# Zeros between the first transposes, one group's first block turned by VectorE, and biases loaded by SyncE: a matmul with bias and tanh

## The chip, the cores and the metric

The kernel runs on one core of one Trainium2 chip. The metric is the device time of one execution in microseconds (us), the median of several executions. One execution of each run was profiled; its **span**, from the first to the last instruction, is about 1.7 us shorter than the time. The **landing** of a transfer is the moment when all of its data has arrived; a **semaphore** is a counter by which a transfer or an engine tells others that it is done.

## The reference

```python
m, k, n = 4096, 4096, 4096
a, b, bias = randn(m, k), randn(k, n), randn(n)     # float32
out = np.tanh(np.matmul(a, b) + bias)
```

## The kernel before

a and b are read as float32 and cast to float16 by the transfer itself, which only GpSimd's queue issues here. TensorE needs a turned (k on the partitions). In the steady state VectorE turns it in 32x32 blocks; the loads put the right 32 partitions into the right place, so each such load is four transfers (`for q in (0, 2, 1, 3)`).

The beginning is built apart, so that TensorE has something to multiply soon. Eight blocks of 128 rows of a are worked on at once: group 0 (`g0`) and group 1 (`g1`), four blocks each, over a first stretch of k (4 rows of 128, `BL`), then a second (4 to 8), then a third (8 to 16). The blocks that are needed first are loaded naturally, one transfer each, and turned on TensorE against an identity matrix:

```python
def load_nat(m):                      # one transfer, 128 KB as float16
    ...
    nc.gpsimd.dma_start(out=nat, in_=src.rearrange("m (x t) -> m x t", t=BL))

def turn_nat(m, copy):                # four transposes, then a copy out of PSUM
    tp = psum.tile([P, BL, P], fp16, name="tp", tag="ps")
    for t in range(BL):
        nc.tensor.transpose(tp[:, t, :], nats[m][:, :, t], ident)
    copy(ats[m][:, ds(0, BL), :], tp)
```

PSUM is the memory that TensorE writes to. Before these transposes TensorE multiplies zeros nine times: they are meant to bring its clock from half to full early. Then (cut):

```python
turn_nat(0, nc.vector.tensor_copy)
turn_nat(1, nc.scalar.copy)
row(0, 0, 1)                          # block 0, first row of b: two matmuls
turn_nat(2, nc.vector.tensor_copy)
row(1, 0, 1)
row(2, 0, 1)
row(0, 1, 1)
...
load_nat(G)                           # group 1, blocks 0 and 1: natural
load_nat(G + 1)
want_a("g1a", 2, 6 * P, 2 * Q, 0, BL) # blocks 2 and 3: 4 transfers of 64 KB
want_a("g1b", G, 4 * P, G * Q, BL, BL)# second stretch of k: 4 of 128 KB
for i in range(BL):
    want(load_b_next)                 # second stretch of b: 4 of 256 KB
want_a("g0b", G, 0, G * Q, BL, BL)    # group 0, second stretch
want_a("g0c", G, 0, G * Q, KS, KM - KS)  # group 0, third stretch
```

`want` puts a load into a list, and at most three loads of a (`AN`) are under way or unturned at a time.

Of the kernel before, what the change touches and what calls it, by code (L numbers as in the profile page):

```python
# [14 lines left out]
P = 128  # L15
Q = 4
QP = 32
NB = 512
fp32 = mybir.dt.float32
# [4 lines left out]
def kernel(  # L24
# [7 lines left out]
    nc = tc.nc  # L32
# [6 lines left out]
    NCW = 1024  # L39
    NC = N // NCW  # L40
    J = NCW // NB
    TB = 4
    G = 4
    KS = 8
    AN = 3
    BL = 4
    KM = 16
    WARM = 9

    singles = ctx.enter_context(tc.tile_pool(name="singles", bufs=1))  # L50
    bpool = ctx.enter_context(tc.tile_pool(name="bpool", bufs=2))
# [4 lines left out]
    psum = ctx.enter_context(tc.tile_pool(name="psum", bufs=8, space=bass.MemoryType.PSUM))  # L56
# [4 lines left out]
    def new_b():  # L61
        return [
            bpool.tile([P, TB, NCW], fp16, name=f"b_{i}", tag=f"b_{i}") for i in range(KT // TB)
        ]
# [19 lines left out]
    def load_a(m0, nmb, t0, nt):  # L84
        an = anat.tile([P, nmb, nt * QP], fp16, name="an")
        for t, n in split(t0, nt):
            for q in (0, 2, 1, 3):
                k = t * P + q * BL * QP if t < KS else P * KS + (q * (KT - KS) + t - KS) * QP
                src = a[ds(m0, nmb * QP), ds(k, n * QP)]
                nc.gpsimd.dma_start(  # L90
                    out=an[ds(q * QP, QP), :, ds((t - t0) * QP, n * QP)],
                    in_=src.rearrange("(mb p) k -> p mb k", p=QP),
                )
        return an

    def transpose_a(at, an, mb0, t0, nt):

        for t, n in split(t0, nt):
            order = "P mb (k t) -> P mb t k" if t < KS else "P mb (t k) -> P mb t k"
            nc.vector.transpose(  # L100
                at[:, ds(t, n), :].rearrange("P t (mb p) -> P mb t p", p=QP),
                an[:, ds(mb0, Q), ds((t - t0) * QP, n * QP)].rearrange(order, k=QP),
            )

    def load_bias(bias_bc, n0, queue):
        src = bias[ds(n0, NCW)]
        queue.dma_start(
            out=bias_bc,
            in_=bass.AP(tensor=src.tensor, offset=src.offset, ap=[[0, P], *src.ap]),
        )  # L110
# [4 lines left out]
    def pump():  # L115
        while queue and (queue[0][0] is None or live[0] < AN):
            key, uses, load = queue.pop(0)
            made = load()
            if key is not None:
                live[0] += 1  # L120
                staged[key] = [made, uses]

    def want_a(key, uses, *where):
        queue.append((key, uses, lambda: load_a(*where)))

    def want(load):
        queue.append((None, 0, load))

    def turn(at, key, mb0, t0, nt):
        pump()  # L130
        transpose_a(at, staged[key][0], mb0, t0, nt)
        staged[key][1] -= 1
        if not staged[key][1]:
            live[0] -= 1
            pump()

    def mm(ps, at, bt, t, j, start, stop):
        nc.tensor.matmul(  # L138
            ps, at[:, t, :], bt[t // TB][:, t % TB, ts(j, NB)], start=start, stop=stop
        )  # L140

    def finish(ps, addend, mi, c0, w=NB, o_sb=None, queues=(nc.sync,)):
# [22 lines left out]
    ats = [  # L165
        bpool.tile([P, KT, P], fp16, name=f"atx_{m}", tag=f"b_{4 + m}") for m in range(G)
    ] + [atp.tile([P, KT, P], fp16, name="at") for m in range(G)]
# [24 lines left out]



    def one_by_one(ps, ms, t0, t1, first, before=None):
        for m in ms:
            if before:
                before(m)
            ps[m] = [psum.tile([P, NB], fp32, name="ps") for j in range(J)]
            for j in range(J):  # L200
                for t in range(t0, t1):
                    mm(ps[m][j], ats[m], b_cur, t, j, t == first, False)

    def across(ps, ms, t0, t1, first):
        for t in range(t0, t1):
            for m in ms:
                for j in range(J):
                    mm(ps[m][j], ats[m], b_cur, t, j, t == first, False)

    def down(ps, ms, t0, t1, done, before=None):  # L210
        for m in ms:
            if before:
                before(m)
            for j in range(J):
                for t in range(t0, t1):
                    mm(ps[m][j], ats[m], b_cur, t, j, False, t == t1 - 1)
                done(ps[m][j], m, j)

    g0, g1 = range(G), range(G, 2 * G)


    zeros = singles.tile([P, NB], fp16, name="zeros")
    ident = singles.tile([P, P], fp16, name="ident")
    nc.vector.memset(zeros, 0.0)  # L224
    nc.vector.memset(ident, 1.0)
    warm = psum.tile([P, NB], fp32, name="ps")
    for i in range(WARM):
        nc.tensor.matmul(warm, zeros[:, :P], zeros, start=i == 0, stop=i == WARM - 1)  # L228



# [6 lines left out]
    def load_nat(m):  # L238
        nat = opool.tile([P, P, BL], fp16, name="nat", tag="o_sb")
        src = a[ds(m * P, P), ds(0, P * BL)]  # L240
        nc.gpsimd.dma_start(out=nat, in_=src.rearrange("m (x t) -> m x t", t=BL))  # L241
        nats[m] = nat
# [6 lines left out]
    def turn_nat(m, copy):  # L249
# [4 lines that stand above are left out]
# [13 lines left out]
    ps = {}  # L267

    def row(m, t0, nt):
        if m not in ps:  # L270
            ps[m] = [psum.tile([P, NB], fp32, name="ps") for j in range(J)]
        across(ps, (m,), t0, t0 + nt, 0)

    turn_nat(0, nc.vector.tensor_copy)
    turn_nat(1, nc.scalar.copy)
    row(0, 0, 1)
    turn_nat(2, nc.vector.tensor_copy)
    row(1, 0, 1)
    row(2, 0, 1)
    row(0, 1, 1)  # L280
    row(1, 1, 1)
    turn_nat(3, nc.scalar.copy)
# [2 lines left out]
    across(ps, g0, 2, BL - 1, 0)  # L285


    load_nat(G)
    load_nat(G + 1)
    want_a("g1a", 2, 6 * P, 2 * Q, 0, BL)  # L290
    want_a("g1b", G, 4 * P, G * Q, BL, BL)
    for i in range(BL):
        want(load_b_next)
# [6 lines left out]
    bias_bc = biasp.tile([P, NCW], fp32, name="bias_bc")  # L300
# [8 lines left out]
    pump()  # L309


    def before0(m):
        if m == 3:
            turn_nat(G, nc.vector.tensor_copy)

    down(ps, g0, BL - 1, BL, put_aside, before0)

    def before1(m):
        if m == G + 1:
            turn_nat(m, nc.vector.tensor_copy)  # L320
            for i in range(2):
                turn(ats[G + 2 + i], "g1a", i * Q, 0, BL)
            for i in range(G):
                turn(ats[G + i], "g1b", i * Q, BL, BL)

    ps = {}
    one_by_one(ps, g1, 0, BL, 0, before1)
    across(ps, g1, BL, KS - 1, 0)
    for m in g0:
        turn(ats[m], "g0b", m * Q, BL, BL)  # L330
# [3 lines left out]
    ps = {}  # L334
# [11 lines left out]
    ps = {}  # L346
# [15 lines left out]
    def want_row(i):  # L362
        want_a(i, 1, todo[i][1] * P, Q, 0, KT)
# [9 lines left out]
    for m in g0:  # L373
        for j in range(J):
            ps = psum.tile([P, NB], fp32, name="ps")
# [10 lines left out]
    bias_next = None  # L386
    for i, (c, mi) in enumerate(todo):
        if mi == 0:
            b_cur, bias_bc = b_next, bias_next
        if c + 1 < NC and mi == (2 * G if c == 0 else 0):  # L390
            b_next = new_b()
            left = [(s, None) for s in range(KS // TB)]
            left += [(s, q) for s in range(KS // TB, KT // TB) for q in range(Q)]
        if i + ahead < len(todo):
            want_row(i + ahead)
        for s, q in left[:2]:
            if q is None:
                want(lambda s=s, c=c, bt=b_next: load_b_low(
                    nc.gpsimd, bt[s], (c + 1) * NCW, s * TB, TB))
            else:  # L400
                want(lambda s=s, q=q, c=c, bt=b_next: load_b(
                    bt, (c + 1) * NCW, s * TB, TB, q))
        left = left[2:]
        if c + 1 < NC and mi == MT - 4:
            bias_next = biasp.tile([P, NCW], fp32, name="bias_bc")
            want(lambda c=c, bb=bias_next: load_bias(bb, (c + 1) * NCW, nc.gpsimd))
        pump()
        if i + 2 < len(todo):
            new_at(i + 2)
        at = at_q.pop(0)  # L410
        for j in range(J):

            halves = 2 if i == len(todo) - 1 and j == J - 1 else 1
            w = NB // halves
            for h in range(halves):
                ps = psum.tile([P, w], fp32, name="ps")
                c0 = j * NB + h * w
                for t in range(KT):
                    nc.tensor.matmul(  # L419
                        ps,  # L420
                        at[:, t, :],
                        b_cur[t // TB][:, t % TB, ds(c0, w)],
                        start=t == 0,
                        stop=t == KT - 1,
                    )
                queues = (nc.sync, nc.scalar) if halves > 1 else (nc.sync,)
                finish(ps, bias_bc[:, ds(c0, w)], mi, c * NCW + c0, w, queues=queues)
# [30 lines left out]
```

## Time and profile before

| what | value |
|---|---|
| time, median of 3 executions | 1783.76 us (1782.66 to 1784.04) |
| span of the profiled one | 1782.8 us (its time was 1784.52, above all three) |
| TensorE busy | 1776.4 us |
| first matmul of group 1 | 16.74 us |
| its first on the second stretch of k | 24.58 us |
| first matmul of the main loop | 121.27 us |

The prediction below shows the lines of TensorE (start, busy us, engine, line, operation, how many; in brackets its idle time before and who ended it).

```profile
6.79 1.18 POOL L241 DMA_DIRECT2D nat<-in_a_dram  x2 [1.24 <-PE tp L252]
7.96 2.32 POOL L90 DMA_DIRECT2D an<-in_a_dram  x4
10.70 0.64 POOL L90 DMA_DIRECT2D an<-in_a_dram  x1 [0.43 <-DMA b<-in_b_dram]
11.95 2.08 POOL L90 DMA_DIRECT2D an<-in_a_dram  x3 [0.60 <-DMA b<-in_b_dram]
14.02 2.16 POOL L69 DMA_DIRECT2D b<-in_b_dram  x4
```

Between the last row of b of the first stretch (issued at 4.99) and the load of group 1's second stretch (from 10.70) stand six issues. Two of the brackets say that GpSimd waited for the *landing* of a row of b before it issued a piece of a that has nothing to do with b. And the work of all engines in stretches of 2 us (length; busy us of TensorE, its weight loads, VectorE, ScalarE and GpSimd, with the number of instructions in brackets; the share of the clock granted, the DMA share, and GB/s):

```profile
14.00:16.00 2.00, 2.00 (x13) 0.96 (x11) 0.00 (x0) 1.04 (x3) 2.00 (x5) 1.00 1.81 178
16.00:18.00 2.00, 1.91 (x12) 0.76 (x11) 0.42 (x1) 2.00 (x6) 2.00 (x4) 1.00 1.38 205
18.00:20.00 2.00, 1.48 (x10) 0.74 (x9) 1.10 (x3) 0.97 (x2) 0.77 (x2) 1.00 1.13 211
```

The transfers move 178 to 211 GB/s.

### The profile page before, as it was taken

What the parts mean: (1) busy time and instruction counts of PE and PEld (TensorE: products, weight loads), DVE (VectorE), ACT (ScalarE), POOL (GpSimd) and SP (SyncE); (2) the same over time, 40 slices, a digit from 0 to 9 for tenths busy, and PEclk for the clock granted to TensorE, in tenths of its full rate; (3) what the DMA queues carried; (4) which work ended last, traced back from release to release, by engine and by line L of the source; (5) the groups of instructions that cost most, each with busy time, mean ns of one, the idle gap of its engine ahead of it and who ended that gap; (6) DMA issues with size and microseconds to landing.
All of it is one profiled execution on the core that took longest, in us unless ns stands there. A gap on an engine that the chain in (4) does not pass through costs nothing.

```text
span 1782.8 us, 20849 instructions
## 1 busy us (share of the span) xinstructions
PE 1776.4 (100%) x8257; PEld 807.8 (45%) x8257; DVE 763.5 (43%) x679; ACT 173.2 (10%) x279; POOL 869.9 (49%) x1620
## 2 busy tenths in 40 slices
PE   9999999999999999999999999999999999999999
PEld 4444444444444444444444444444444444444444
DVE  2764443344434443444434443444334443444342
ACT  2021000000000000000000000000000000000001
POOL 7465556544466445444455554444544454444510
PEclk9999999999999999999999999999999999999999
DMA  9999999976999967767699987766777667766631
GB/s 188 201 184 175 169 162 167 138 133 107 159 168 163 161 109 117 119 109 128 112 167 173 167 142 117 120 116 107 129 116 122 107 112 117 119 114 109 117 77 42
DMA packets 280593, 238.68 MB, mean 134 GB/s; under 512 B 158000, under 2 KB 230960, under 8 KB 280496
## 3 DMA queue, kind: packets, MB, share of 16 engines
q0 software_dynamic: 243056, 169.71, 69.4%
q1 hardware_dynamic: 37152, 67.52, 10.6%
q8 instruction: 64, 1.05, 0.2%
q14 instruction: 33, 0.27, 0.0%
q10 hardware_dynamic: 288, 0.13, 0.0%
HBM read 337.64 MB, written 67.11 MB: 227 GB/s over the span
## 4 chain that ended last, share of the span: by engine, by line
PE 99%; DMA 0%; issue 0%; ACT 0%; DVE 0%; DVEq 0%; POOLq 0%
PE ps L419 93%; PE ps L138 6%; DMA nat<-in_a_dram 0%; PE tp L252 0%; ACT o_sb L152 0%; DVE at L253 0%; DVE o_sb L149 0%; ACT atx L253 0%; DVEq L149 0%; POOLq L442 0%
## 5 line engine op out<-in xcount | busy, mean ns | idle before, releaser
L419 PE MATMUL ps<-b,at 128*128 128x512 f16 x7712 | 1657.8, 378 | 0.0
L90 POOL DMA_DIRECT2D an<-in_a_dram x1488 | 800.2, 545 | 794.9 <-DVE at L100 562.4
L419 PEld LDWEIGHTS <-at 128*128 128x128 f16 x7712 | 754.6, 98 | 903.3
L100 DVE STREAM_TRANSPOSE at<-an 128x512 f16<-128x512 f16 (+1 forms) x378 | 564.0, 1543 | 54.9 <-DMA an<-in_a_dram 54.8
L149 DVE TENSOR_TENSOR o_sb<-ps,bias_bc 128x512 f32<-128x512 f32 (+1 forms) x243 | 165.9, 684 | 917.6 <-PE ps L419 712.3
L152 ACT ACTIVATE o_sb<-o_sb 128x512 f32<-128x512 f32 (+1 forms) x243 | 151.6, 625 | 1502.5 <-DVE o_sb L149 1496.2
L73 POOL DMA_DIRECT2D b<-in_b_dram x104 | 56.0, 541 | 20.6 <-DMA an<-in_a_dram 11.7
L138 PE MATMUL ps<-b,atx 128*128 128x512 f16 x256 | 57.7, 385 | 0.2 <-ACT atx L253 0.2
L138 PE MATMUL ps<-b,at 128*128 128x512 f16 x256 | 55.8, 379 | 0.6 <-DVE at L253 0.5
L138 PEld LDWEIGHTS <-at 128*128 128x128 f16 x256 | 24.9, 98 | 31.0 <-DVE at L253 1.3
L138 PEld LDWEIGHTS <-atx 128*128 128x128 f16 x256 | 25.0, 99 | 30.6 <-ACT atx L253 0.7
L100 DVE STREAM_TRANSPOSE atx<-an 128x512 f16<-128x512 f16 (+2 forms) x12 | 16.3, 1398 | 9.3 <-DMA an<-in_a_dram 9.3
L69 POOL DMA_DIRECT2D b<-in_b_dram x13 | 8.3, 643 | 20.1 <-PE ps L419 19.8
L152 ACT ACTIVATE spill<-spill 128x512 f32<-128x512 f32 x16 | 10.1, 629 | 81.8 <-DVE spill L149 81.8
L149 DVE TENSOR_TENSOR spill<-ps,spill 128x512 f32<-128x512 f32 x16 | 11.0, 686 | 13.3 <-PE ps L138 13.3
L181 DVE TENSOR_TENSOR spill<-spill,bias_bc 128x512 f32<-128x512 f32 x16 | 9.7, 677 | 0.0
L173 ACT COPY spill<-ps 128x512 f32<-128x512 f32 x16 | 8.0, 626 | 14.3 <-PE ps L138 14.3
L176 DVE TENSOR_TENSOR spill<-ps,spill 128x512 f32<-128x512 f32 x8 | 4.9, 681 | 4.0 <-PE ps L138 4.0
L228 PE MATMUL ps<-zeros 128*128 128x512 f16 x9 | 4.0, 631 | 1.3 <-DVE zeros L224 1.3
L253 DVE COPY at<-tp 128x512 f16<-128x512 f16 x2 | 0.8, 424 | 9.5 <-PE tp L252 9.5
L241 POOL DMA_DIRECT2D nat<-in_a_dram x6 | 3.4, 564 | 2.2 <-PE tp L252 1.2
L253 DVE COPY atx<-tp 128x512 f16<-128x512 f16 x2 | 0.8, 424 | 6.7 <-PE tp L252 6.7
(14 smaller groups left out, 13.3 us busy)
## 6 DMA issues: line engine op xcount, KB each, us to landing
an<-in_a_dram POOLq DMA_DIRECT2D x480, 192.0 KB, 4.9
out_dram<-o_sb SPq DMA_DIRECT2D x239, 256.0 KB, 2.5
an<-in_a_dram POOLq DMA_DIRECT2D x960, 32.0 KB, 2.6
b<-in_b_dram POOLq DMA_DIRECT2D x95, 256.0 KB, 8.1
b<-in_b_dram POOLq DMA_DIRECT2D x6, 1024.0 KB, 13.4
an<-in_a_dram POOLq DMA_DIRECT2D x32, 128.0 KB, 5.0
out_dram<-spill SPq DMA_DIRECT2D x16, 256.0 KB, 3.5
an<-in_a_dram POOLq DMA_DIRECT2D x12, 256.0 KB, 8.5
```

Of the source, the lines that this page charges most:

```text
L69: queue.dma_start(out=dst, in_=src[:, ds(t0 % BL, nt), :])
L73: nc.gpsimd.dma_start(out=bt[t0 // TB][ds(q * QP, QP), ds(t0 % TB, nt), :], in_=src.rearrange("(t p) n -> p t n", p=QP),)
L90: nc.gpsimd.dma_start(out=an[ds(q * QP, QP), :, ds((t - t0) * QP, n * QP)], in_=src.rearrange("(mb p) k -> p mb k", p=QP),)
L100: nc.vector.transpose(at[:, ds(t, n), :].rearrange("P t (mb p) -> P mb t p", p=QP), an[:, ds(mb0, Q), ds((t - t0) * QP, n * QP)].rearrange ...
L138: nc.tensor.matmul(ps, at[:, t, :], bt[t // TB][:, t % TB, ts(j, NB)], start=start, stop=stop)
L149: nc.vector.tensor_tensor(out=o_sb[:, piece], in0=ps[:, piece], in1=addend[:, piece], op=mybir.AluOpType.add)
L152: nc.scalar.activation(o_sb[:, piece], o_sb[:, piece], mybir.ActivationFunctionType.Tanh)
L173: nc.scalar.copy(aside(m, j), ps)
L176: nc.vector.tensor_tensor(out=aside(m, j), in0=ps, in1=aside(m, j), op=mybir.AluOpType.add)
L181: nc.vector.tensor_tensor(out=aside(m, j), in0=aside(m, j), in1=bias_bc[:, ts(j, NB)], op=mybir.AluOpType.add)
L228: nc.tensor.matmul(warm, zeros[:, :P], zeros, start=i == 0, stop=i == WARM - 1)
L419: nc.tensor.matmul(ps, at[:, t, :], b_cur[t // TB][:, t % TB, ds(c0, w)], start=t == 0, stop=t == KT - 1,)
```

## The change

Three things are meant. More zeros, also between the first transposes and matmuls, so that TensorE has no hole and its clock opens early. Group 1's first four blocks turned by VectorE out of two loads, so that TensorE loses no time to their transposes and to the copies after them. The three later biases loaded through SyncE's queue, the first of them in two halves.

```diff
-    WARM = 9
+    WARM = 11
...
+    def fill(n, w):
+        ps = psum.tile([P, NB], fp32, name="ps")
+        for i in range(n):
+            nc.tensor.matmul(
+                ps[:, ds(0, w)], zeros[:, :P], zeros[:, :w], start=i == 0, stop=i == n - 1
+            )
+    fill(WARM, NB)
...
     turn_nat(0, nc.vector.tensor_copy)
+    fill(3, P)
     turn_nat(1, nc.scalar.copy)
     row(0, 0, 1)
+    fill(2, P)
     turn_nat(2, nc.vector.tensor_copy)
     row(1, 0, 1)
+    fill(3, P)
     row(2, 0, 1)
+    fill(6, P)
     row(0, 1, 1)
...
-    load_nat(G)
-    load_nat(G + 1)
-    want_a("g1a", 2, 6 * P, 2 * Q, 0, BL)
+    want_a("g1a", 2, 4 * P, 2 * Q, 0, BL)
+    want_a("g1a2", 2, 6 * P, 2 * Q, 0, BL)
     want_a("g1b", G, 4 * P, G * Q, BL, BL)
...
+    for i in range(G):
+        turn(ats[G + i], "g1a2" if i > 1 else "g1a", i % 2 * Q, 0, BL)
     ...  (the two turn_nat between group 1's matmuls are gone)
-            want(lambda c=c, bb=bias_next: load_bias(bb, (c + 1) * NCW, nc.gpsimd))
+            for h in range(2 if c == 0 else 1):
+                w = NCW // (2 if c == 0 else 1)
+                load_bias(bias_next[:, ds(h * w, w)], (c + 1) * NCW + h * w, nc.sync)
```

More of the change, by code (lines that the diff above doesn't have):

```diff
@@ L105, in load_bias @@
     def load_bias(bias_bc, n0, queue):
-        src = bias[ds(n0, NCW)]
+        src = bias[ds(n0, bias_bc.shape[-1])]
         queue.dma_start(
@@ L190, in load_b_all, with one_by_one @@
             load_b(b_cur, 0, t0, nt, q)
-    def one_by_one(ps, ms, t0, t1, first, before=None):
+    def one_by_one(ps, ms, t0, t1, first):
         for m in ms:
-            if before:
-                before(m)
-            ps[m] = [psum.tile([P, NB], fp32, name="ps") for j in range(J)]
+            ps[m] = []
             for j in range(J):
+                ps[m].append(psum.tile([P, NB], fp32, name="ps"))
                 for t in range(t0, t1):
@@ L208, in across, with down @@
                     mm(ps[m][j], ats[m], b_cur, t, j, t == first, False)
-    def down(ps, ms, t0, t1, done, before=None):
+    def down(ps, ms, t0, t1, done):
         for m in ms:
-            if before:
-                before(m)
             for j in range(J):
@@ L225 @@
     nc.vector.memset(ident, 1.0)
-    warm = psum.tile([P, NB], fp32, name="ps")
-    for i in range(WARM):
-        nc.tensor.matmul(warm, zeros[:, :P], zeros, start=i == 0, stop=i == WARM - 1)
+    def fill(n, w):
[5 more added lines that the diff above has]
+    fill(WARM, NB)
     raw_b = spill[3].rearrange("P (t x) n -> P t (x n)", t=2)[:, ds(0, 1), :]
@@ L309 @@
     pump()
-    def before0(m):
-        if m == 3:
-            turn_nat(G, nc.vector.tensor_copy)
-    down(ps, g0, BL - 1, BL, put_aside, before0)
-    def before1(m):
-        if m == G + 1:
-            turn_nat(m, nc.vector.tensor_copy)
-            for i in range(2):
-                turn(ats[G + 2 + i], "g1a", i * Q, 0, BL)
-            for i in range(G):
-                turn(ats[G + i], "g1b", i * Q, BL, BL)
+    for i in range(G):
+        turn(ats[G + i], "g1a2" if i > 1 else "g1a", i % 2 * Q, 0, BL)
+    down(ps, g0, BL - 1, BL, put_aside)
+    for i in range(G):
+        turn(ats[G + i], "g1b", i * Q, BL, BL)
     ps = {}
-    one_by_one(ps, g1, 0, BL, 0, before1)
+    one_by_one(ps, g1, 0, BL, 0)
     across(ps, g1, BL, KS - 1, 0)
```

## The prediction

> **What bounds the kernel now.** I read the page from the top. TensorE is busy for 1776.4 of 1782.8 us, and the chain of waits that ended last is 99% TensorE.
>
> ```profile
> PE 1776.4 (100%) x8257; PEld 807.8 (45%) x8257; DVE 763.5 (43%) x679; ACT 173.2 (10%) x279; POOL 869.9 (49%) x1620
> ...
> PE 99%; DMA 0%; issue 0%; ACT 0%; DVE 0%; DVEq 0%; POOLq 0%
> ```
>
> So no transfer and no other engine can give much. Is there anything to win on TensorE itself? The chain in order of time answers (columns: start, length in us, what).
>
> ```profile
> 1.31 4.51 DMA nat<-in_a_dram
> ...
> 5.87 0.62 PE tp L252 x4
> ...
> 8.47 2.57 PE ps L138 x8
> ...
> 11.30 0.59 ACT atx L253
> ...
> 16.26 0.44 DVE at L253
> ...
> 18.90 0.43 DVE at L253
> ...
> 19.39 102.05 PE ps L138 x472
> 121.43 1654.20 PE ps L419 x7680
> ```
>
> From 19.39 us on TensorE never waits: 1654.20 us for 7680 matmuls is 215.4 ns each, and in the trace no matmul after 20 us starts more than 217 ns behind the one before it. The last 7.2 us (1775.6 to 1782.8) are the adds, tanh and stores of the last tile, which the change doesn't touch. The whole program has 8192 matmuls of the product (256 + 256 + 7680 and the few halves at the end), at 215.4 ns about 1765 us. With 5.87 us of waiting for the first block of a and 7.2 us of tail that is 1778 us; some 5 us at most lie in the beginning, and **only those can be won**. The TensorE timeline of the beginning (start, busy us, what, idle before):
>
> ```profile
> 1.26 4.02 PE L228 MATMUL ps<-zeros 128*128 128x512 f16 x9 [1.26 <-DVE zeros L224]
> 5.87 1.26 PE L252 MATMUL tp<-ident,nat 128*128 128x128 f16 x8 [0.59 <-DMA nat<-in_a_dram]
> ...
> 8.26 2.77 PE L138 MATMUL ps<-b,atx 128*128 128x512 f16 x8
> ...
> 11.94 4.06 PE L138 MATMUL ps<-b,atx 128*128 128x512 f16 x18 [0.25 <-ACT atx L253]
> 15.84 0.39 PE L252 MATMUL tp<-ident,nat 128*128 128x128 f16 x4
> 16.06 0.59 PE L138 MATMUL ps<-b,atx 128*128 128x512 f16 x2
> 16.74 1.90 PE L138 MATMUL ps<-b,at 128*128 128x512 f16 x8
> 18.48 0.39 PE L252 MATMUL tp<-ident,nat 128*128 128x128 f16 x4
> 19.39 12.26 PE L138 MATMUL ps<-b,at 128*128 128x512 f16 x56 [0.52 <-DVE at L253]
> ```
>
> Two losses are in it. First, speed: the 18 matmuls from 11.94 take 0.216 us each, the ones on zeros start 0.427 us apart, and single starts in the trace show the change of pace inside the matmul that starts at 9.97, near 10.06 us. All work between 5.87 and 10.06 ran at half pace. Second, group 1's first two blocks are turned on TensorE in the middle of the matmuls (15.84 and 18.48): four transposes each, then a wait for VectorE's copy out of PSUM.
>
> **What the Trainium skill says.** "TensorE: Matmul & The Clock Gate", section "What's actually happening": the array starts at half clock and gets the full one after a busy window of about 3.4 us; the window is free-running. The trace agrees: the pace doubles at 10.06, and the 3.41 us before it (6.65 to 10.06) have no gap, while the window before that (3.24 to 6.65) holds the hole from 5.08, where the last zeros stop streaming, to 5.87. Section "Wait — 56ns, not 53.3ns?": starts are 106.7 and 426.7 ns apart at N = 128 and 512 cold, 55.6 and 215.7 warm. The trace has 107 and 427, then 56 and 216. "VectorE: DVE Perf Modes", section "The three transpose paths": VectorE turns 32x32 blocks only, into SBUF. That is why the change also swaps the loads; the trace has 6 such turns of 128x512 in 3.67 us, 0.61 each, with no PSUM copy. "DMA: Bandwidth & Descriptors", section "Issuing engines are not separate DMA queues": another issuing engine saves only issue time. That bears on the bias.
>
> **The change part by part.** The order of instructions shows TensorE with 8 more pairs: +2 zeros of 512 columns, +14 of 128, -8 transposes. The rest of its order is the same.
>
> *Zeros.* Eleven at 0.427 from 1.26 end at 5.95, against the first block of a landing at 5.83: 0.08 us late, but no hole. The small ones stand where TensorE would wait for a landing or for a copy of a transpose (0.42 us on VectorE, 0.58 on ScalarE). With the same phase of the window, the window 3.24 to 6.65 is now busy throughout, so the full clock comes at about 6.65 instead of 10.06. I then walked the new order by hand with the landings of the trace before (blocks of a at 5.83, 6.47, 7.26, 9.16; rows of b at 8.52, 10.42, 11.66), the copies' durations, and about 0.05 us for a semaphore: transposes of block 0 5.95 to 6.38, zeros, block 1 6.68 to 6.90, first matmuls at 7.10 (the copy of block 0 ends at 7.05), block 2 at 7.64, block 1's matmuls 7.87, block 2's 8.55, six zeros from 8.98, then the second row of b at 9.31 against 9.97 before. The six zeros cost 0.33 us there, since that row has landed at 8.52. Block 3's copy by ScalarE still has to be waited for: its first matmul comes at about 11.23 against 11.94. **Saved: 0.7 us.**
>
> *Group 1 on VectorE.* From 11.23 there are 4 + 8 + 8 matmuls, 20 x 0.216 = 4.32 us, and group 1 starts at 15.55. Before it started at 16.74: the four transposes (4 x 0.056 = 0.22) and the wait (0.25) are gone, 0.48 us. The second block before cost from the end of the eighth matmul (18.48) to 19.39, 0.91 us. **Saved: 1.4 us**, if the turned blocks are ready. VectorE needs 0.61 us a block and is idle from 8.93. The loads are the question. The queue of GpSimd is full here, and landings come one behind the other at its pace: in the trace the last row of b at 11.66, the two blocks that go (128 KB each) at 12.32 and 13.10, the 64 KB pieces of the remaining load 0.38 us apart, to 14.47. The new loads are the same bytes in eight such pieces: 11.66 + 4 x 0.38 = 13.2 for the first two blocks, 14.7 for the others. Turned by 14.4 and 15.9; needed at 15.55 and, two blocks x 1.73 us later, at 19.0. Margin over one us.
>
> *What comes sooner must be fed sooner.* Group 1's second block of K: landed 17.50 before, needed at 15.55 + 32 x 0.216 = 22.5. Group 0's next load: 26.18, turned by 26.8, needed at 29.4. Its third: 31.41, turned from 32.7, needed at 36.3; the b for it lands by 33.97. Later b at 60.29, needed at 63.9; the load of a at 70.64, turned by 71.9, needed at 77.7. All hold with over a us, so the gain should reach the end.
>
> *Biases.* Three issues of 0.56 us leave GpSimd, which idles 794.9 us at its loads; four go to SyncE, which waits 1555 us for ScalarE. TensorE waits for neither: **0**.
>
> Sum: 24.57 before for the first matmul of group 1 on the second block of K, 22.46 after: 2.1 us off the profiled span, 1780.7.
>
> **The rivals.** (1) *The zeros bring no earlier clock*, because zeros of 128 columns or transposes count too little or a hole stays. Then 14 zeros at 0.107 are 1.5 us of load at half pace, part of it in gaps, and the zeros eat most of the gain: about 1783. For it: nothing in the trace shows zeros alone opening the clock. Against: the window 6.65 to 10.06 opened it with eight transposes' worth of time inside. (2) *The loads become the wait*: 32-partition pieces are issued at 0.58 us each, and each issue reuses a semaphore of an earlier DMA, so two of them wait for rows of b (10.42, 11.66). A late load of group 1 would put a DMA wait where the VectorE wait was, at 15.55 or 22.5; each us late costs one us, 1782 to 1783. Against: the queue's pace, not the issue, sets the landings there. (3) *The phase of the window favours the change more*: before, it can open anywhere from 9.3 to 12.7, after from 4.7 to 8.1. Walked by hand this moves before by -0.1 to +1.1 and after by only -0.3 to +0.5. For it: the three runs before spread over 1.4 us. The usual run before is then somewhat later than the profiled one, and the gain 2.5 to 2.8: 1781.0.
>
> **Range and chances.** 1783.76 - 2.1 = 1781.7 by the profiled phase, 1781.0 by the usual one; I take 1781.2. The low end is a gain of 3.7 (a late clock before in the median, an early one after), the high end 1.1 (rival 1 or 2 in part). Two per cent is 36 us, and the beginning holds about 5: anything but "within 2%" would need a fault elsewhere.
>
> **What would show it.** Weight loads about 0.22 us apart from about 6.7 us on; no idle TensorE between 1.3 and 5.9; no VectorE copies into group 1's tiles; group 1's first matmul near 15.6, with no wait before its second block; the first matmul of the main loop near 119.2 instead of 121.27; 215.4 ns a matmul there as before; no wait at L107. Wrong would be a DMA wait of TensorE at 15 to 30 us, or a pace of 0.43 us still at 9 us.

## The result

| | before | changed |
|---|---|---|
| time, median | 1783.80 us (1782.66 to 1784.04, 4 runs) | 1783.83 us (1783.25 to 1784.13, 4 runs) |
| ratio | | 1.0001, 95% interval 0.9984 to 1.0018 |
| span of the profiled run | 1782.8 | 1781.9 |

Ratios here are the mean time of one kernel's runs over that of the other's runs of the same rounds, so not quite the ratio of the medians quoted. The time stayed where it was; the predicted 1781.2, with a range of 1780.0 to 1782.7, was missed on the high side.

The page of the changed kernel, busy time by engine and the chain that ended last:

```profile
PE 1775.9 (100%) x8265; PEld 807.2 (45%) x8265; DVE 763.6 (43%) x679; ACT 173.1 (10%) x279; POOL 869.2 (49%) x1619
...
PE 97%; DMA 1%; POOL 0%; DVE 0%; issue 0%; ACT 0%; DVEq 0%; POOLq 0%
```

The eight more pairs of weight load and matmul on TensorE are there as the order said. The chain was 99% TensorE before; now 1%, some 24 us, runs through transfers (0.9% b, 0.4% a). TensorE's timeline:

```profile
1.26 4.57 PE L228 MATMUL ps<-zeros 128*128 128x512 f16 x11 [1.26 <-DVE zeros L221]
...
15.17 14.38 PE L138 MATMUL ps<-b,at 128*128 128x512 f16 x64
29.84 8.69 PE L138 MATMUL ps<-b,atx 128*128 128x512 f16 x38 [0.29 <-DVE atx L100]
39.05 12.69 PE L138 MATMUL ps<-b,atx 128*128 128x512 f16 x58 [0.52 <-DVE atx L100]
```

The front came out a little better than predicted, with some luck: the first block of a landed at 5.16 and the clock opened at 5.40, where the prediction had 5.83 and 6.65. Group 1 starts at 15.17 (predicted 15.55, before 16.74) with no transposes inside it, and is at its second stretch of k at 22.27 (predicted 22.46, before 24.58): 2.3 us ahead. But the main loop starts at 120.64, only 0.63 us ahead of 121.27. Between lie new waits: single starts in the trace show 0.41 us lost around 22 to 24 us, 0.46 at 29.8, 0.30 at 37.0, 0.71 at 38 to 39: 1.88 us in all. Before had none of that after 20 us. VectorE is named as the releaser, but what did VectorE wait for? The chain in order of time:

```profile
5.00 7.25 DMA b<-in_b_dram
...
12.53 3.11 POOL an L90 x5
15.64 1.54 POOL b L69 x3
...
17.24 8.73 DMA b<-in_b_dram
...
26.25 7.99 DMA an<-in_a_dram
...
34.37 4.63 DVE atx L100 x4
...
39.05 81.76 PE ps L138 x378
```

Before 39 us the chain no longer runs through TensorE. It runs through a landing of b (12.24), then GpSimd's issues one after another, then a landing of b again, then of a. GpSimd's timeline shows how:

```profile
5.52 2.33 POOL L90 DMA_DIRECT2D an<-in_a_dram  x4
8.84 0.58 POOL L90 DMA_DIRECT2D an<-in_a_dram  x1 [1.00 <-DMA b<-in_b_dram]
9.99 0.58 POOL L90 DMA_DIRECT2D an<-in_a_dram  x1 [0.57 <-DMA nat<-in_a_dram]
11.24 0.58 POOL L90 DMA_DIRECT2D an<-in_a_dram  x1 [0.68 <-DMA b<-in_b_dram]
12.53 3.11 POOL L90 DMA_DIRECT2D an<-in_a_dram  x5 [0.71 <-DMA b<-in_b_dram]
```

The compiled order of GpSimd's instructions says why: each transfer signals one of eight semaphores in turn, and carries a wait for the transfer eight before it on the same semaphore. The second small load's four pieces therefore wait for the landings of a row of b (8.56), block 3 of a (9.71) and two more rows of b (10.96, 12.24); each is issued 0.28 us after such a landing. Eight issues now stand where six stood, and the load of group 1's second stretch is issued from 13.09 instead of 10.70. Since the pieces are 64 KB, there is then less under way (at 15 us, 576 KB had been issued and not landed, against 1024 KB before), and the rate falls:

```profile
14.00:16.00 2.00, 2.00 (x11) 0.88 (x9) 1.90 (x3) 2.00 (x5) 2.00 (x4) 1.00 1.12 104
16.00:18.00 2.00, 2.00 (x11) 0.91 (x10) 0.69 (x2) 1.87 (x4) 2.00 (x5) 1.00 1.32 122
18.00:20.00 2.00, 2.00 (x11) 0.94 (x10) 0.00 (x0) 0.00 (x0) 1.09 (x2) 1.00 1.22 130
```

104 to 130 GB/s where before moved 178 to 211. Everything behind lands late by about three us: group 1's second stretch at 21.0 instead of 17.5, group 0's third at 34.2 instead of 31.4 (by 2.4 and 2.1 us against a second profile of before, below).

Late issue is only part of it. The last piece of group 1's second stretch was issued at 14.99 instead of 13.39, and then took 6.0 us to land instead of 4.1. At 17.5 us as much had been issued and not landed in both kernels (1408 KB), and yet the rate was 122 and 130 GB/s from 16 to 20 us, against 205 and 211. What held these transfers up is not shown.

### The profile page after: what moved, and what is told of

It is laid out like the page before. It is cut to its first block, busy times and chain, and to the rows that moved or that the text cites. A ratio compares the mean times of both kernels' runs of the same rounds, so it can differ in the third digit from the quotient of the medians. Undisturbed runs are those within 1.5% of the kernel's fastest.

```text
span 1781.9 us, 20875 instructions
## 1 busy us (share of the span) xinstructions
PE 1775.9 (100%) x8265; PEld 807.2 (45%) x8265; DVE 763.6 (43%) x679; ACT 173.1 (10%) x279; POOL 869.2 (49%) x1619
## 4 chain that ended last, share of the span: by engine, by line
PE 97%; DMA 1%; POOL 0%; DVE 0%; issue 0%; ACT 0%; DVEq 0%; POOLq 0%
PE ps L419 93%; PE ps L138 5%; DMA b<-in_b_dram 1%; DMA an<-in_a_dram 0%; DVE atx L100 0%; POOL an L90 0%; POOL b L69 0%; POOL nat L245 0%; ACT o_sb L152 0%; DVE o_sb L149 0%; POOL ident L262 0%; POOLq L262 0%; DVEq L100 0%; DVEq L149 0%; POOLq L442 0%
## 5 line engine op out<-in xcount | busy, mean ns | idle before, releaser
L73 POOL DMA_DIRECT2D b<-in_b_dram x104 | 56.0, 542 | 15.7 <-DMA an<-in_a_dram 8.5
L138 PEld LDWEIGHTS <-atx 128*128 128x128 f16 x256 | 24.4, 98 | 31.7 <-DVE atx L100 2.7
L228 PE MATMUL ps<-zeros 128*128 128x128 f16 (+1 forms) x25 | 6.0, 387 | 1.3 <-DVE zeros L221 1.3
```

What stands on the lines that cost most here:

```text
L73: nc.gpsimd.dma_start(out=bt[t0 // TB][ds(q * QP, QP), ds(t0 % TB, nt), :], in_=src.rearrange("(t p) n -> p t n", p=QP),)
L138: nc.tensor.matmul(ps, at[:, t, :], bt[t // TB][:, t % TB, ts(j, NB)], start=start, stop=stop)
L228: nc.tensor.matmul(ps[:, ds(0, w)], zeros[:, :P], zeros[:, :w], start=i == 0, stop=i == n - 1)
```

## The experiments

The theory to be tested, called **S** in the expectations: more and smaller issues, under a limit of eight, starve the transfers, and the late landings eat what TensorE gained. No run changed the limit or the time that GpSimd takes for one issue (0.52 to 0.68 us), so the runs test the number and size of the issues, and not which of these two makes them costly. Rivals: the late landings have another cause (the size of packets, transfers at their limit, chance); the zeros gain nothing (C); the profiled run of before was not a usual one, because the clock opened late in it (P).

What each profile showed. "Clock" is where the trace's record of the full granted clock begins; "g1" the first matmul of group 1; "lands" the last pieces of group 1's second and of group 0's third stretch; "waits" the time lost between matmuls from 20 us on; "loop" the first matmul of the main loop. The times are medians, with that of before in the same rounds.

| run | clock | g1 | lands | waits | loop | time | before |
|---|---|---|---|---|---|---|---|
| before | 10.04 | 16.74 | 17.5, 31.4 | 0 | 121.27 | 1783.80 | |
| before_again | 5.66 | 15.86 | 18.6, 32.2 | 0 | 120.38 | 1783.63 | 1783.99 |
| changed | 5.40 | 15.17 | 21.0, 34.2 | 1.88 | 120.64 | 1783.83 | 1783.80 |
| after_again | 4.80 | 14.77 | 20.4, 33.9 | 1.90 | 120.27 | 1783.33 | 1783.62 |
| zeros_only | 7.25 | 16.13 | 17.7, 31.7 | 0 | 120.66 | 1784.56 | 1783.99 |
| turn_only | 5.27 | 15.62 | 20.1, 34.2 | 1.37 | 120.59 | 1784.74 | 1783.99 |
| one_load | 5.74 | 17.27 | 19.4, 32.6 | 0 | 120.88 | 1783.74 | 1783.99 |
| one_load_turn | 4.48 | 16.66 | 19.0, 31.9 | 0 | 120.27 | 1783.50 | 1783.96 |
| before_split | 5.66 | 15.82 | 21.2, 36.3 | 2.26 | 122.59 | 1785.83 | 1783.96 |
| small_later | 5.17 | 15.66 | 16.9, 33.5 | 0.5 | 120.06 | 1782.96 | 1783.96 |
| small_later_9 | 4.65 | 15.18 | 16.8, 33.5 | 0.7 | 120.09 | 1782.90 | 1783.62 |
| small_later_b2 | 6.81 | 16.94 | 17.8, 35.0 | 0.9 | 121.44 | 1783.66 | 1783.62 |
| no_zeros | 10.84 | 16.97 | 18.7, 33.1 | 0 | 121.50 | 1784.73 | 1783.96 |
| bias_only | 4.88 | 15.68 | 17.7, 31.8 | 0 | 120.20 | 1783.15 | 1783.62 |

Every 95% interval of a ratio includes 1, so each verdict rests on what the profile shows, which is one profile a run, and the times go along with it or not.

A rival that no run was made for is the limit of three loads of a (`AN`), since the change makes two loads of one. The trace of the changed kernel speaks against it: from 12.53 to 18.42 us GpSimd issues one transfer after another, and its first wait for VectorE to turn a load ends at 22.77, some 0.3 us after the landing of a row of b (22.22) would have let it go on.

### before_again: the kernel before once more

> The kernel before, unchanged, once more: how far do two sets of runs of one kernel differ, and where does the clock open in a second profile? Theory P (the free-running window sits differently, and the usual run of before opens the clock earlier than the profiled one did, at 10.06 us): the second profile opens it elsewhere, and its span moves by half the difference. Theory S (nothing of that, the loads ate the gain): the profile is as before, first matmul of group 1 at 16.7 us, first of its second block of K at 24.6, no wait of TensorE after 20 us. Ratio to before 1.000 within 0.0005 in either.

1783.63 us, ratio 0.9999 (0.9987 to 1.0012). The clock opened at 5.66 instead of 10.04, and all came about 0.9 us earlier. TensorE's timeline:

```profile
5.69 0.41 PE L252 MATMUL tp<-ident,nat 128*128 128x128 f16 x4 [0.41 <-DMA nat<-in_a_dram]
...
15.86 1.90 PE L138 MATMUL ps<-b,at 128*128 128x512 f16 x8
```

Four transposes of 128 columns in 0.41 us (before: 0.62) are at full pace, at 5.69 us. Of the seven profiles with nine zeros here (before, before_again, turn_only, one_load_turn, before_split, small_later_9, bias_only) six have the clock open by 5.7 us; the first one, on which the prediction was built, is the exception. Theory P holds, in the sense opposite to the one the prediction gave it: rival 3 had the clock of the kernel before opening from 9.3 us on. Against this usual run of before, the changed kernel is 0.69 us ahead at group 1's start and 1.42 ahead at its second stretch (23.69 to 22.27), and 0.26 us *behind* at the main loop.

### zeros_only

```diff
 kernel before
+    WARM = 11 and fill(3), fill(2), fill(3), fill(6) as in the change
```

> Only the zeros, on the kernel before: group 1's first two blocks stay on TensorE and the loads stay as they were. Theory S (the gain was real, and the two loads in quarters gave it back by starving the transfers): group 1's first matmul about 1 us earlier than in before, near 15.7, no DMA wait of TensorE later, landings as in before (17.5 us for group 1's second block of K, 26.2 for group 0's), and the main loop starts about 1.0 us earlier than 121.3: time 0.7 to 1.2 us under before. Theory C (the zeros gain nothing that lasts): the main loop starts at 121.3 all the same.

1784.56 us against 1783.99, ratio 1.0003 (0.9990 to 1.0015). Neither expectation was met. The landings are those of before and there is no late wait, as S had it. But the clock opened only at 7.25 here, and the loop starts at 120.66: 0.6 us before the first profile of before, 0.3 us behind the second. The zeros gained nothing over a usual run of before. The span of this profile is also lengthened at the very end: its last stores landed 0.8 us later after the last matmul than in every other profile (3.62 against 2.80); that is not from the zeros' place in the program, and why it happened stays open.

### turn_only

```diff
 changed kernel
-    WARM = 11, the four fill(...) between, biases by SyncE
+    WARM = 9, none between, biases as before
```

> Only the turning on VectorE with its two loads, on the kernel before (9 zeros, none between; biases as before). Theory S: the transfers starve as in the changed kernel, group 1's second block of K lands at about 21 us instead of 17.5 and group 0's at about 29, and TensorE, which comes about 1.4 us earlier than before to group 1's second block, waits there and at group 0's third block (36 to 39 us) by 0.5 to 1.5 us in all: time within 0.5 us of before or somewhat above. Rival theory (TensorE came too early for transfers that were not slower): landings at 17.5 and 26.2 as before, no wait, 1.4 us faster.

1784.74 us, ratio 1.0002 (0.9990 to 1.0015). The starved stretch is there without any added zeros: landings at 20.1 and 34.2, waits of 1.37 us. So the loads cause it, not the zeros. Against before_again, which also has nine zeros, group 1 is 1.16 us ahead at its second stretch (23.69 to 22.53): that is about what turning on VectorE gains by itself.

### one_load

```diff
 changed kernel
-    want_a("g1a", 2, 4 * P, 2 * Q, 0, BL)
-    want_a("g1a2", 2, 6 * P, 2 * Q, 0, BL)
+    want_a("g1a", G, 4 * P, G * Q, 0, BL)
```

> The changed kernel with one edit: group 1's first four blocks of a in one load of four pieces of 128 KB instead of two loads of four pieces of 64 KB each. The bytes and their order are the same, but four issues fewer stand between the first rows of b and the rest. Theory S (each issue waits for the landing of the one eight before it, so eight small pieces leave too few bytes under way): GpSimd issues group 1's second block of K from about 9 us instead of 13.1, the rate between 12 and 20 us goes from 104 to 148 back to 175 to 210 GB/s, it lands near 18 us instead of 21, group 0's third block near 31.5 instead of 34.2, the waits of TensorE at 22 to 39 us (1.9 us in all in the changed kernel) shrink to under 0.5, and the time falls by 1.2 to 2 us below the changed kernel's, to about 1782. Group 1 may start a little later, up to 15.7 instead of 15.17, for its first block lands with all four. Rival theory (the transfers are at their limit and TensorE comes too early for them): the landings stay late, and so does the time.

1783.74 us, ratio 0.9998 (0.9984 to 1.0011). Half of it came: the rate from 12 to 20 us was 177 to 211 GB/s, group 1's second stretch landed at 19.4, group 0's third at 32.6, and there was no wait after 20 us. But the time did not fall. The expectation allowed group 1 a start of up to 15.7; it was 17.27, for two reasons that TensorE's timeline names:

```profile
10.29 1.02 PE L138 MATMUL ps<-b,atx 128*128 128x512 f16 x4 [1.14 <-DMA b<-in_b_dram]
...
17.27 1.04 PE L138 MATMUL ps<-b,at 128*128 128x512 f16 x4 [0.57 <-DVE at L100]
```

The second row of b landed at 10.24 (8.5 to 9.6 in most other profiles), and group 1's four blocks were all turned only after their whole load was in. The waits moved to the front.

### before_split: the suspected cost alone, on the kernel before

```diff
 kernel before
-    want_a("g1a", 2, 6 * P, 2 * Q, 0, BL)       # four pieces of 64 KB
+    want_a("g1a", 1, 6 * P, Q, 0, BL)           # eight pieces of 32 KB
+    want_a("g1a2", 1, 7 * P, Q, 0, BL)
```

> The kernel before, with its one load of two blocks of a (four pieces of 64 KB) cut into two loads of one block (eight pieces of 32 KB); nothing else. Theory S (an issue waits for the landing of the one eight before it, so more and smaller issues leave fewer bytes under way): the rate falls to under 150 KB/us for some us after 12 us, the second block of K of group 1 lands 1.5 to 3.5 us later than 17.5, and the later loads stay late by as much; group 1's second block then has TensorE waiting, or the waits come at group 0's second and third loads (29 to 39 us): time 0.3 to 1.5 us over before. Rival (the small packets or the order of the bytes made the changed kernel's loads slow, not the number of issues): packets and order are as before here, so landings and time stay.

1785.83 us against 1783.96, ratio 1.0011 (0.9998 to 1.0023); all five runs (1785.04 to 1787.04) are above all nine of before (1783.32 to 1784.83). That is more than the 1.5 us that the expectation allowed. The bytes and the packets are the same, in nearly the same order, in four issues more; GpSimd's timeline has them, and the stretches of 2 us the rate:

```profile
12.46 4.39 POOL L90 DMA_DIRECT2D an<-in_a_dram  x7 [0.71 <-DMA b<-in_b_dram]
12.00:14.00 2.00, 2.00 (x11) 0.88 (x9) 0.00 (x0) 0.00 (x0) 1.33 (x3) 1.00 1.29 144
14.00:16.00 2.00, 1.91 (x13) 0.84 (x11) 0.42 (x1) 1.96 (x5) 2.00 (x4) 1.00 0.50 45
16.00:18.00 2.00, 1.94 (x12) 0.93 (x10) 0.02 (x1) 2.00 (x5) 2.00 (x5) 1.00 1.53 137
```

And TensorE's timeline of the same run:

```profile
26.00 5.34 PE L138 MATMUL ps<-b,at 128*128 128x512 f16 x24 [0.43 <-DMA b<-in_b_dram]
```

45 GB/s in the worst 2 us, landings at 21.2 and 36.3, and TensorE waits for b itself, at a pace that before could feed. More and smaller issues alone are enough to make the loads late; this is the clearest run. It does not separate the limit of eight from the time of an issue: the load of group 1's second stretch is issued 3.6 us later than in before (14.29 against 10.70), and four more issues take about 2.2 us of GpSimd by themselves.

### small_later: same issues, larger ones first

```diff
 changed kernel
     want_a("g1a", 2, 4 * P, 2 * Q, 0, BL)
-    want_a("g1a2", 2, 6 * P, 2 * Q, 0, BL)
     want_a("g1b", G, 4 * P, G * Q, BL, BL)
+    want_a("g1a2", 2, 6 * P, 2 * Q, 0, BL)
```

> The changed kernel with one edit: the second of the two loads in 64 KB pieces is asked for after the load of group 1's second block of K (four pieces of 128 KB) instead of before it. The same number of issues and the same bytes, but the larger ones go first. Theory S: the rate between 12 and 20 us comes back to 160 or more, group 1's second block of K lands by 18 us, group 0's third load near 32 instead of 34.2, and the waits of 1.9 us in the changed kernel shrink to under 0.8; a new short wait may come at group 1's third block, near 18.6, whose load now lands at about 18. Time 0.5 to 1.2 us below the changed kernel's 1783.8. Rival: no change.

1782.96 us against 1783.96, ratio 0.9993 (0.9979 to 1.0007); four of the five runs are below all nine of before in the same rounds. The rate, in stretches of 2 us:

```profile
14.00:16.00 2.00, 2.00 (x11) 0.91 (x10) 1.30 (x2) 1.65 (x4) 2.00 (x4) 1.00 1.72 168
16.00:18.00 2.00, 2.00 (x11) 0.88 (x9) 0.00 (x0) 2.00 (x5) 1.89 (x5) 1.00 1.41 136
```

168 and 136 against 104 and 122. Group 1's second stretch lands at 16.9 instead of 21.0. Group 0's third lands at 33.5, later than the 32 expected, and a wait of 0.3 us before 38.3 is left; one of 0.3 us before 19.4 came as expected, outside the table's column. With the same issues, swapping two lines of the list takes the waits after 20 us from 1.9 to 0.5 us. The small pieces, now issued from 13.39 on without any wait, still come with a fall to 136 GB/s at 16 to 18 us, which suggests that the time of an issue counts too (64 KB each 0.57 us is 115 GB/s, an estimate).

The profile shows less of a gain than the times. The main loop starts at 120.06, 0.3 us ahead of before_again and 0.1 ahead of bias_only, whose beginning is that of before; another 0.24 us come at the end (bias_only, below). The rest of the 1.0 us is not shown.

### one_load_turn, small_later_9, small_later_b2

```diff
 one_load_turn:  one_load, with 9 zeros and none between, biases as before
 small_later_9:  small_later, with 9 zeros and none between
 small_later_b2: small_later, and b's second four rows two to an issue (512 KB)
```

> The kernel before with group 1's first block turned by VectorE out of one load of 128 KB pieces, 9 zeros and none between. In the changed kernel with one load the rows of b landed 1.4 to 1.7 us later than in any other profile (10.2 instead of 8.5 to 9.3 for the first of them), which ate what the later landings gained. Theory L (the large pieces, issued at 5.5 to 8 us behind the rows of b, slow these down themselves): the rows of b land late again, 10 us or more for the first, and the time is that of before within 0.5 us. Theory N (it was the scatter of one run): they land at 8.5 to 9.3, no wait of TensorE after 20 us, time 1.0 to 1.5 us under before.

1783.50 us against 1783.96. Neither theory came out clean: the second row of b landed at 9.39, inside the scatter, yet the last of its first four only at 12.85 (before: 11.66 and 12.24), and group 1, whose blocks come in one load, started at 16.66, after a wait of 0.81 us for VectorE. No wait after 20 us. Whether large pieces issued behind the rows of b slow these down stays open: in small_later_b2, which has small pieces there, the second row landed at 10.17 as well.

> The changed kernel with the small pieces asked for later (which took 1.0 us off before), and now with 9 zeros at the start and none between, as in before: what are the added zeros worth where the loads no longer eat the gain? If they make the clock open early more often: this is 0.3 to 0.8 us slower than with them (about 1783.4 to 1783.8), with some runs a us slower than others. If nine zeros open the clock as often, or the landings of b's rows (8.5 to 13 us) set the beginning anyway: within 0.3 us of 1782.96.

1782.90 us against 1783.62, 0.7 us less, where small_later had 1.0; with five runs each, over 1 us apart, that is the same. The added zeros are worth nothing that these runs show. The six profiles with eleven zeros have the clock open at 4.80 to 7.25, none as late as 10.04; whether they guard against a late clock now and then would take more profiles.

> The changed kernel with the small pieces asked for later and, besides, b's second four rows loaded two to an issue (512 KB) instead of one. Theory S says that what is left (the rate falls to 95 KB/us at 17 us, waits of 0.3 us at 18.9 and 37.8) comes of GpSimd issuing one small piece after another from 12.5 us on: with two issues fewer behind them, the later loads are issued about 1.1 us earlier and group 0's third load lands before 33 us instead of 33.5; the wait at 37.8 goes, that at 18.9 stays: 0.2 to 0.4 us below small_later, about 1782.6. A wait for b's rows at 22 us would be the price, since two rows land together.

1783.66 us, equal to before. A miss. The price that the expectation named was paid: the two rows landed together at 24.6 and TensorE waited 0.74 us for them; and in the profiled run the first rows were late besides. That fewer issues here would help is not shown.

### no_zeros, bias_only, after_again

```diff
 no_zeros:    kernel before without its nine matmuls on zeros
 bias_only:   kernel before with load_bias(..., nc.sync) as in the change
 after_again: the changed kernel, unchanged
```

> The kernel before without its nine matmuls on zeros: what is the clock of the beginning worth? All work from 5.87 us on then runs at half pace until a busy window is over, at 9.3 us at the earliest. If the clock mattered as the prediction had it, half a us is lost for each us that it opens later, and the time is 0.7 to 1.5 us over before, whose clock opened at 10.0 in one profile and at 5.7 in the other. If the transfers set the pace of the beginning anyway, the loss is under 0.4 us.

1784.73 us against 1783.96. The clock opened at 10.84 and the loop started at 121.50, 1.1 us behind before_again. The late clock goes with a late start, as the prediction said, though the second row of b was late here as well (9.62); the nine zeros already win the clock, most of the time.

> The kernel before with only the third part of the change: the three later biases loaded by SyncE, the first of them in two halves. Every theory: nothing, within 0.3 us of before, since TensorE waits for no bias and GpSimd idles at its loads; no wait at the add of the bias.

1783.15 us against 1783.62, ratio 0.9998 (0.9984 to 1.0011). Not quite nothing. From the last store's landing to the end of the span this profile, like every other one with biases on SyncE, needs 0.92 us; those with biases on GpSimd need 1.16. At the end SyncE checks the semaphores of the stores one after another, 0.06 us each. Four more transfers on its queue move the last two stores from the middle of that list to its end, so that the other checks are over when the stores land. That is 0.24 us, at the tail, by the order of a list.

> The changed kernel, unchanged, once more, beside the runs below on the same chip. Theory S: the same starved stretch, under 150 KB/us for several us between 13 and 20 us, group 1's second block of K landing near 21 us, group 0's third load near 34, and 1.5 to 2.2 us of waits of TensorE between 21 and 40 us; time 1783.3 to 1784.2. If the late landings of the first profile were chance, the waits are gone here.

1783.33 us, ratio 1.0000 (0.9987 to 1.0012). Landings at 20.4 and 33.9, waits of 1.90 us, 117 and 127 GB/s from 14 to 18 us: the starved stretch was not chance.

## Why the prediction was wrong, point by point

*What bounds the kernel* was right: some five us at the beginning were all there was, and the main loop ran at the same pace in both kernels. Its sum holds through two errors that nearly cancel. The last 7.2 us are not adds, tanh and stores alone: TensorE multiplies until 1779.1. And 215.4 ns is a mean that includes 32 matmuls of half width; a whole one takes 215.8. So it is 8192 x 0.2158 = 1768 us, 5.87 at the start and 3.7 at the end, 1777.5 in place of 1778.

*The zeros, 0.7 us:* the mechanism was right, the size was not. The clock did open early in the changed kernel (5.40 and 4.80). But the step "saved: 0.7 us" compared with a clock at 10.04, and rival 3 guessed that the usual run of before opens even later. Six of seven profiles with nine zeros opened by 5.7 us. What the term measured is zero, within what these profiles can tell: zeros_only gained nothing on before_again, and small_later_9 equals small_later within the scatter. With eleven zeros rival 3 had the clock at 4.7 to 8.1 us, and all six profiles lie there; with nine it had 9.3 to 12.7, and six of seven lie outside.

*Group 1 on VectorE, 1.4 us:* the mechanism was right, at its place. Against before_again, with nearly the same clock, the changed kernel is 0.69 us ahead at group 1's start and 1.42 at its second stretch, a wait of 0.19 just before that already taken off; turn_only, without the zeros, is 0.24 and 1.16 ahead.

*The step that failed* is "What comes sooner must be fed sooner", with its "all hold with over a us". It took the landings of the trace before as given. Rival 2 had the right place to look, "each issue reuses a semaphore of an earlier DMA", but only for the load of group 1's first stretch, which came in time (by 15.26, needed for its last two blocks at 18.6); the loads behind it were late. It dismissed the point with "the queue's pace, not the issue, sets the landings there". That was true of before, with six issues in that place and whole blocks of 128 KB among them. With eight small ones the pace itself fell, from 178 to 104 GB/s at 14 to 16 us, and the landings slipped by three us (two against before_again). TensorE then waited 1.88 us: 1.42 + 0.19 gained, 1.88 lost, so 0.27 us behind before_again, and the trace has 0.26. The walk looked at *when* loads were needed and at *how many bytes* lay ahead, not at how many issues may be under way.

*The biases, 0:* TensorE indeed waits for none. The 0.24 us at the end were not foreseen.

*In sum:* predicted gain 2.6 us on the median; 1.9 were lost to the late loads, and most of the rest was a gain over a run of before that was not a usual one. The prediction took the gain off the median of 1783.76, but had worked it out on a profiled run of 1784.52; its span of 1780.7 would be 1782.4 as a time. The one edit that feeds the loads better, small_later, is 1.0 us faster than before in its rounds, of which the profiles account for 0.4 to 0.6.

## What to carry to other kernels

When a load is cut into more pieces, count the issues that may be under way as well as the bytes: where every issue waits for the one eight before it and takes over half a us itself, as here, small pieces in a critical stretch can lower the rate for all that stands behind them, and putting the larger ones first took most of the waits away. A gain of a few us measured from one profile of a kernel whose clock opens by chance needs a second profile of the kernel *before*. And work that moves forward needs its feed checked under the new order of issues, not under the old landings.

## What the Trainium skill lacked or had wrong

- "TensorE: Matmul & The Clock Gate", "What's actually happening": it gives one busy window of about 3.4 us, sustained. It does not say how busy. The record's stretches of full clock are 1771.5, 1774.9 or 1778.3 us long, 3.4 us apart. If windows of 3.41 us end where the clock opened, one that held a hole opened it (before_again: 2.25 to 5.66, zeros streaming until 5.08, 83% busy), while windows of 70% (before, 3.22 to 6.63) and 76% (zeros_only, 0.43 to 3.84) did not. The threshold between them is worked out from three profiles.
- The same section says that the window is free-running and varies the transition by about half a us, and a note in it counts 6 to 14 cold matmuls, which at 0.427 us each would be 2.6 to 6.0 us (an estimate). Here, with nine zeros and a hole, the opening varied from 3.2 to 8.8 us after the first matmul at 1.26 (4.48 to 10.04 us), and the main loop's start with it by 1.1 us (120.20 in bias_only to 121.27 in before, whose landings are alike).
- "DMA: Bandwidth & Descriptors", "Anatomy of one DMA — SWDGE (gpsimd) path": its fit, 2.0 us plus bytes over 436e3, gives an estimate of 2.3 us for a piece of 128 KB. Here such a load takes longer from issue to landing. The first one of the kernel before, with nothing ahead of it on GpSimd's queue, took 4.5 us (1.31 to 5.83); a piece in the starved stretch of the changed kernel, with others ahead of it, took 4.05 (13.09 to 17.14), and 3.3 in after_again. All of these are cast on the way; no run here shows how much of the difference that makes.
- No page that bears on this has the limit of eight issues under way on GpSimd's queue as this kernel is compiled. With more and smaller issues the rate at 14 to 16 us was 104 instead of 178 GB/s, and 45 in before_split; the share of the limit in that is not separated.
- No page has the order in which SyncE checks the stores' semaphores at the end; it is worth 0.24 us here.
